# First mixer of a four-block trunk: u projected before the latents, S5 states beside the products of queries, keys and values

## Chip, cores, metric

One core of one Trainium2 chip. The metric is the device time of one execution in microseconds (us), the median of the runs shown.

## What is computed

Two layers, each a half-weighted feed-forward, a mixer, and another half-weighted feed-forward, on 256 tokens of width 1024. Only the mixer of layer 0 is changed. It projects the normalised input to u (512 columns), the query latent (384), the key and value latent (256) and a rotary key (32), and joins an S5 recurrence over u with a causal attention of 8 heads:

```python
def _even_mixer(h, cos_m, sin_m, w_in, ...):
    proj = h @ w_in
    u, c_q, c_kv, k_rope = jnp.split(proj, [S5_WIDTH, ...], axis=-1)
    s5_out = _s5(u, ...)      # states x_t = a x_{t-1} + B u_t; y = Re(C x) + D u; gelu, gate
    q = (_rmsnorm(c_q, q_norm) @ w_uq)...      # 8 heads of 64 + 32 rotary
    kv = (_rmsnorm(c_kv, kv_norm) @ w_ukv)...  # 8 heads of 64 + 64
    ...
    o = _causal_attention(q_full, k_full, v)
    return jnp.concatenate([s5_out, o], axis=-1) @ w_out
```

## The kernel before

Everything is float32, computed as three products of float32r halves: each operand is split into `hi` and `lo`, and hi·hi, hi·lo and lo·hi are summed in PSUM. Weights are split on the chip. `Weights.pre` (L54 to L73) makes one chunk: ScalarE (ACT) copies a staged piece to `whi` (L69), VectorE (DVE) subtracts it to get `wlo` (L71), and SyncE issues the load of a later piece (L50). In the first mixer there are four wide buffers, two chunks' worth, so a chunk can only be split once TensorE (PE) has finished with the chunk two places ahead of it in the list `mix0`.

The order on each engine is fixed when the program is built, by a scheduler that works from the order in which the code issues; at run time each engine takes its instructions in that order. The mixer `mixer0` issues, in this order:

- `cq` and `ckv`, the latents (48 products each), then `pu`, the projection of u (48 products). `low_rank` normalises the latents: a square with a sum on ACT, one step on DVE, a power on GpSimd (POOL), a product on DVE. `latents` transposes them between the two halves of `pu`.
- `queries(0)` and `keys_values(0)`: the products of heads 0 to 3 (18 on `pq`, 12 on `pk`), with u's blocks turned to the S5 layout between them (`uT`, `u`: 8 transposes on PE, copies on ACT and DVE).
- `block_inputs`: 32 products that bring u into the S5 states' space (`v_re`, `v_im`), for two halves b = 0 and 1 of the 16 pairs of S5 groups.
- `heads_turned(0)`: 16 transposes and the copies `qT` (DVE) and `kT` (ACT), without which no score can begin; then the first scores, and `states(b)` in pieces between `queries(1)`, `keys_values(1)` and the first two heads.
- `states(b)`: on DVE 6 products and sums, 2 scans and 3 more products and sums (`z_re`, `z_im`, `t`, `xs_re`); on POOL 3 operations (`xs_im`). `outputs(b)`: 24 products `yp` that need `xs_re` and `xs_im` of that half. `gelu(b)` follows, then the gate and the output projection.

`attend(h)` issues the scores of head h+2 and the values of head h: three transposes of the exponentials, a copy `pT` on ACT, three products.

Of the kernel before, what the change touches and what calls it, by code (L numbers as in the profile page):

```python
# [29 lines left out]
class Weights:  # L30
    """A stream of weight chunks: loaded ahead, each split exactly into two float32r parts."""
# [22 lines left out]
    def pre(self, other=None):  # L54
        """Splits the next chunk; other: an engine that helps with its second half."""
# [32 lines left out]
def trunk(ctx: ExitStack, tc: tile.TileContext, x, pos, invf, wff, gains, w_u, w_cq, w_ckv,  # L88
# [42 lines left out]
    def behind_both(last):  # L131
        """Work that is issued after two instructions on their engines."""
# [25 lines left out]
    mix0 = [(w, True) for w in (w_cq[0], w_cq[1], w_ckv[0], w_ckv[1], w_u[0], w_u[1], w_uq[0], w_ukv[0], w_uq[1],  # L158
# [9 lines left out]
    def rsqrt(out, a):  # L168
        """out = a ** -0.5, one column or more."""
        nc.gpsimd.tensor_tensor(out=out, in0=a, in1=mhalf[:, :a.shape[1]], op=ALU.pow)  # L170
# [13 lines left out]
    def transpose_split(src, nk, hi, lo, t):  # L184
        """token-major src [128, nk*128] -> feature-major halves, columns of token tile t."""
# [9 lines left out]
    # Phases hand the residual stream over one token tile at a time: a phase's last products for tile 0  # L195
    # come first, and those for tile 1 run while tile 0 is normalised for the next phase.
# [67 lines left out]
    def ffn(prev, row, background=None):  # L264
# [25 lines left out]
        # the first two feature tiles, one token tile at a time  # L290
# [73 lines left out]
    def sincos(ang, cos, sin, n, tmp):  # L364
        """cos and sin of ang [128, n] by an exact reduction to [-pi, pi]."""
# [19 lines left out]
    # exp by powf: its base is e rounded to float32, which a factor makes good  # L385
# [80 lines left out]
    def rope(v, nh, cc, ss, half, eng=None):  # L466
        """v [128, nh, 2*half] in place."""
# [27 lines left out]
    def s5_prep():  # L495
# [16 lines left out]
        # matrices that are filled last hold intermediates until then  # L512
# [21 lines left out]
        # powers of a and of its direction  # L534
# [21 lines left out]
        # e^{i theta n}, n = 0..63, by doubling  # L556
# [16 lines left out]
        # f = (a - 1) / lambda, bb = f B  # L573
# [31 lines left out]
        # inputs to states: E_i = a^{3-i} bb, and their transposes  # L605
# [22 lines left out]
        # states to outputs: W_d = c a^d  # L628
# [38 lines left out]
        # within a block: rows (i', c'), columns (i, c) hold Re(c a^{i-i'} bb), and the skip on the diagonal  # L667
# [12 lines left out]
    def product(acc, t, ws, k0, per, width, hi, lo, nk, cols=None):  # L680
        """token tile t of a product with k-tiles k0.. of the weights, `width` columns"""
# [18 lines left out]
    def row_maxima(sp, s, scale, mx):  # L700
        """masked and scaled scores of two query tiles, and the maxima of their rows"""
# [5 lines left out]
    def row_exps(s, mx, l):  # L707
        """exponentials and their sums; mx: the maxima, negated"""
# [13 lines left out]
    def mixer0(prev):  # L722
# [12 lines left out]
        cq = [bank("cq")[:, :384] for _ in range(2)]  # L735
        c0, c1 = queue.pop(0), queue.pop(0)
        product(cq[0], 0, c0, 0, 4, 384, yh, yl, KT)
        finish()
        product(cq[0], 0, c1, 4, 4, 384, yh, yl, KT)
        product(cq[1], 1, c0, 0, 4, 384, yh, yl, KT)  # L740
        more()
        product(cq[1], 1, c1, 4, 4, 384, yh, yl, KT)
        more()
        cqh, cql = s4("cqh", [128, 3, SEQ], F32R), s4("cql", [128, 3, SEQ], F32R)
        ckh, ckl = s2("ckh", [128, 2, SEQ], F32R), s2("ckl", [128, 2, SEQ], F32R)
        cqy = [low_rank(cq[t], 384, qg[:, :384]) for t in range(2)]
# [9 lines left out]

        ckv = [bank("ckv")[:, :288] for _ in range(2)]
        project(ckv, 288, lambda: None)
# [4 lines left out]

        # u, then blocks of four steps down the partitions
        pu = [bank("pu") for _ in range(2)]

        def latents():
            for t in range(2):
                transpose_split(cqy[t], 3, cqh, cql, t)
            for t in range(2):  # L770
                transpose_split(cky[t], 2, ckh, ckl, t)

        project(pu, 512, latents)
        us = [s2("us", [128, 512]) for _ in range(2)]
        for t in range(2):
            nc.scalar.copy(out=us[t], in_=pu[t])
# [5 lines left out]
        def queries(g):  # L782
# [7 lines left out]
            if g == 0:  # L790
                more()

        def keys_values(g):
# [7 lines left out]
            if g == 0:  # L801
                more()

        queries(0)
# [4 lines left out]
        uT = s4("uT", [128, 4, 4, NBLK])  # L809
        for t in range(2):  # L810
            pt = bank("pt").rearrange("p (k c) -> p k c", c=128)
            for k in range(4):
                nc.tensor.transpose(pt[:, k, :], us[t][:, k * 128:(k + 1) * 128], ident)
            pv = pt.rearrange("p m (n i) -> p m i n", i=4)
            for i in range(4):
                nc.scalar.copy(out=uT[:, :, i, 32 * t:32 * t + 32], in_=pv[:, :, i, :])
        u = s4("u", [128, NPAIR, NBLK])
        uv = u.rearrange("p (m a) n -> p m a n", a=4)
        for a in range(4):
            for i in range(4):  # L820
                dst = uv[32 * i:32 * i + 32, :, a, :]
                src = uT[32 * a:32 * a + 32, :, i, :]
                if i == 3 or i == 1 and a % 2:
                    nc.scalar.copy(out=dst, in_=src)
                else:
                    nc.vector.tensor_copy(out=dst, in_=src)
        keys_values(0)
# [45 lines left out]
        st = [states(b, *v[b]) for b in range(2)]  # L873
        s5e.close()
        att = ExitStack()
# [123 lines left out]
        next(st[0])  # L999
        queries(1)  # L1000
        attend(0)
        next(st[1])
        keys_values(1)
        attend(1)
        for _ in st[0]:
            pass
        heads_turned(1)
        for _ in st[1]:
            pass
        more()  # L1010
        yp = outputs(0)
        attend(2)
        gelu(0, yp)
        attend(3)
        osb = normalised(0)
        attend(4)
        yp = outputs(1)
# [349 lines left out]
```

## Time and profile before

| | us |
|---|---|
| median of 3 runs (1045.62 to 1045.81) | 1045.69 |
| span of the profiled execution, first to last instruction | 1044.7 |
| busy: PE, DVE, ACT, POOL | 1012.1, 635.2, 494.1, 101.4 |
| mean granted TensorE clock | 0.980 |

The profiled execution is of the same program; what of a run lies outside its span is some 1.0 us against the median. PE is busy for 97% of the span, so a shorter time has to come from its idle time or from stretches in which its clock is at the lower of its two levels.

### The profile page before, as it was taken

Reading aid. Unit: us, or ns where it says so; the run is one execution under the profiler, and the core shown is the slowest. Engines: PE = TensorE matmul, PEld = TensorE weight load, DVE = VectorE, ACT = ScalarE, POOL = GpSimd, SP = SyncE. Lnnn points to the kernel's source line nnn. Section 1 sums busy time; section 2 is a strip of 40 time slices with the busy share of each in tenths; the row PEclk is TensorE's granted clock in tenths of the full one; section 3 lists DMA queues with packets and bytes.
Section 4 is the critical chain, followed back from the end, with each engine's and each line's share of the span. In section 5 each row is a group of like instructions: output and inputs, shape, how many; then the busy total and the mean of one; then the engine's idle time right before and its main releaser. Section 6 shows DMA issues by size and latency. Waiting matters only on the chain.

```text
span 1044.7 us, 16739 instructions
## 1 busy us (share of the span) xinstructions
PE 1012.1 (97%) x6730; PEld 928.3 (89%) x6730; DVE 635.2 (61%) x1117; ACT 494.1 (47%) x848; POOL 101.4 (10%) x115
## 2 busy tenths in 40 slices
PE   7999998999979999999999999999999999999997
PEld 6999997989878899999989999999888879999996
DVE  5788778365877865555447455543757776555432
ACT  5454542455636664444336444442567756444431
POOL 3210006601510100000010000000101110000000
PEclk9999997899969999999999999999999999999999
DMA  8866663135113585555627565563453448556521
GB/s 270 262 186 196 189 190 101 51 117 187 61 41 111 192 302 182 182 184 186 209 68 263 168 217 185 189 190 140 143 180 122 143 133 290 184 184 192 187 80 40
DMA packets 49807, 174.93 MB, mean 167 GB/s; under 512 B 6081, under 2 KB 7105, under 8 KB 49730
## 3 DMA queue, kind: packets, MB, share of 16 engines
q1 hardware_dynamic: 48720, 170.46, 50.8%
q10 hardware_dynamic: 1010, 3.41, 0.9%
q8 instruction: 52, 0.85, 0.3%
q14 instruction: 25, 0.20, 0.1%
HBM read 172.80 MB, written 1.05 MB: 166 GB/s over the span
## 4 chain that ended last, share of the span: by engine, by line
PE 85%; DVE 6%; issue 3%; ACT 3%; POOL 1%; DMA 1%; SPq 0%; POOLq 0%; DVEq 0%; ACTq 0%
PE gu L336 43%; PE acc L280 22%; PE proj L685 6%; PE gt L300 3%; DVE wlo L71 2%; PE acc L696 2%; PE pu L685 1%; DVE tmat L118 1%; PE pt L190 1%; DMA xr<-in_x_dram 1%; PE ckv L685 1%; PE pz L976 1%; PE cq L685 1%; PE yp L944 1%; ACT y L199 1%
## 5 line engine op out<-in xcount | busy, mean ns | idle before, releaser
L71 DVE TENSOR_TENSOR wlo<-stage,whi 128x1024 fp32r<-128x1024 f32 x230 | 287.8, 1259 | 244.1 <-ACT whi L69 243.9
L69 ACT CAST whi<-stage 128x1024 fp32r<-128x1024 f32 (+1 forms) x236 | 240.4, 1030 | 292.5 <-issue 237.6
L336 PE MATMUL gu<-yh,whi 128*128 128x256 f32 x1280 | 363.1, 284 | 0.0
L336 PE MATMUL gu<-yh,wlo 128*128 128x256 f32 x1280 | 363.0, 284 | 0.0
L336 PE MATMUL gu<-yl,whi 128*128 128x256 f32 x1280 | 362.8, 283 | 0.0
L336 PEld LDWEIGHTS gu<-yh,whi 128*128 128x128 f32 x1280 | 246.2, 192 | 2.7
L336 PEld LDWEIGHTS gu<-yl,whi 128*128 128x128 f32 x1280 | 246.2, 192 | 2.7
L336 PEld LDWEIGHTS gu<-yh,wlo 128*128 128x128 f32 x1280 | 246.1, 192 | 0.0
L280 PE MATMUL acc<-dhi,hs 128*128 128x512 f32 x704 | 193.7, 394 | 0.0
L280 PEld LDWEIGHTS acc<-dhi,hs 128*128 128x128 f32 x704 | 128.1, 190 | 23.3 <-ACT hs L127 0.3
L71 DVE TENSOR_TENSOR dlo<-stage,dhi 128x1024 fp32r<-128x1024 f32 x88 | 108.3, 1232 | 36.3 <-ACT dhi L69 35.8
L69 ACT CAST dhi<-stage 128x1024 fp32r<-128x1024 f32 x88 | 92.3, 1050 | 68.8 <-DMA stage<-in_wff_dram 68.6
L280 PE MATMUL acc<-dlo,hs 128*128 128x512 f32 x352 | 110.9, 391 | 0.0
L280 PEld LDWEIGHTS acc<-dlo,hs 128*128 128x128 f32 x352 | 66.4, 189 | 14.4
L170 POOL TENSOR_TENSOR rs<-rs,mhalf 128x1 f32<-128x1 f32 x14 | 7.8, 557 | 658.4 <-DVE rs L124 658.4
L118 DVE TENSOR_TENSOR sh<-sh,gu 128x256 f32<-128x256 f32 x80 | 33.1, 414 | 31.8 <-ACT sh L340 31.8
L118 DVE TENSOR_TENSOR hs<-sh,hs 128x256 fp32r<-128x256 f32 x80 | 35.6, 445 | 18.7 <-ACT hs L127 18.6
L340 ACT ACTIVATE sh<-gu 128x256 f32<-128x256 f32 x80 | 30.3, 379 | 31.3 <-PE gu L336 31.3
L127 ACT CAST hs<-sh 128x256 fp32r<-128x256 f32 x80 | 32.3, 403 | 16.9 <-DVE sh L118 16.9
L685 PE MATMUL proj<-whi,yh 128*128 128x512 f32 x96 | 38.7, 403 | 0.2 <-ACT yh L127 0.2
L685 PE MATMUL proj<-wlo,yh 128*128 128x512 f32 x96 | 37.5, 391 | 0.0
L300 PE MATMUL gt<-whi,yh 128*128 128x256 f32 x128 | 34.7, 300 | 2.7 <-ACT yh L127 2.6
(326 smaller groups left out, 1138.7 us busy)
## 6 DMA issues: line engine op xcount, KB each, us to landing
stage<-in_wff_dram SPq DMA_DIRECT2D x264, 512.0 KB, 4.6
stage<-in_w_in_dram SPq DMA_DIRECT2D x24, 512.0 KB, 4.4
stage<-in_w_out_dram SPq DMA_DIRECT2D x16, 512.0 KB, 3.7
gain<-in_gains_dram ACTq DMA_DIRECT2D x6, 512.0 KB, 4.9
stage<-in_w_u_dram SPq DMA_DIRECT2D x4, 512.0 KB, 4.7
xr<-in_x_dram SPq DMA_DIRECT2D x2, 512.0 KB, 5.2
stage<-in_w_cq_dram SPq DMA_DIRECT2D x2, 512.0 KB, 4.1
stage<-in_w_ckv_dram SPq DMA_DIRECT2D x2, 512.0 KB, 4.7
```

Of the source, the lines that this page charges most:

```text
L69: nc.scalar.copy(out=hi[:, c:c + w], in_=t[:, :w])
L71: eng.tensor_tensor(out=lo[:, c:c + w], in0=t[:, :w], in1=hi[:, c:c + w].bitcast(F32), op=ALU.subtract)
L118: return nc.vector.tensor_tensor(out=out, in0=a, in1=b, op=op)
L127: copy = nc.scalar.copy(out=hi, in_=src)
L190: nc.tensor.transpose(pt[:, k, :], src[:, (k0 + k) * 128:(k0 + k + 1) * 128], ident)
L199: return nc.scalar.activation(out=y[:, sl], in_=xr[t][:, sl], func=AF.Square, scale=1.0 / 32.0, accum_out=ms[:, c:c + 1]).ins
L280: nc.tensor.matmul(acc[t][c], a[:, sl], w[:, c * 512:(c + 1) * 512], start=(f == 0 and n == 0), stop=(f == NF - 1 and n == 2))
L300: last = nc.tensor.matmul(o, a[:, k, sl], w[:, k * 256:(k + 1) * 256], start=(k0 == 0 and n == 0), stop=(k0 > 0 and n == 11))
L336: nc.tensor.matmul(gu[:, s * 256:(s + 1) * 256], w[:, k, s, :], a[:, k, :], start=(k == 0 and n == 0), stop=(k == KT - 1 and n == 2))
L340: nc.scalar.activation(out=sh[:, 0, :], in_=gu[:, :256], func=AF.Silu)
L685: last = nc.tensor.matmul(acc, a[:, k0 + k, sl], w[:, k * width:(k + 1) * width], start=(k0 == 0 and n == 0), stop=(k0 + per == nk and n = ...
L696: mm = nc.tensor.matmul(acc[t][c], a[:, k0 + k, sl], w[:, o:o + 512], start=(first and k == 0 and n == 0), stop=(last and k == 1 and n == 2))
```

## The change

No arithmetic is changed. In `mix0` the chunks of u come first. `mixer0` projects u where it projected the query latent, turns u's blocks between the two halves of the `cq` product (`u_blocks`), and turns the query latents between the two halves of the `ckv` product. `block_inputs` then follow the latents, before any query or key product. `states(0)` is issued between `queries(0)` and `keys_values(0)`, `states(1)` between `queries(1)` and `keys_values(1)`, each whole, and only after all of these `heads_turned(0)`. The two calls of `more()` that split the first output chunk and the gate's chunk move up into `queries(1)` and `keys_values(1)`. `outputs(b)` and `gelu(b)` are issued between the first heads. The comments and docstrings that the full difference also removes are left out here.

```diff
-    mix0 = [(w, True) for w in (w_cq[0], w_cq[1], w_ckv[0], w_ckv[1], w_u[0], w_u[1], w_uq[0], w_ukv[0], w_uq[1],
+    mix0 = [(w, True) for w in (w_u[0], w_u[1], w_cq[0], w_cq[1], w_ckv[0], w_ckv[1], w_uq[0], w_ukv[0], w_uq[1],
...
-        cq = [bank("cq")[:, :384] for _ in range(2)]
+        pu = [bank("pu") for _ in range(2)]
         c0, c1 = queue.pop(0), queue.pop(0)
-        product(cq[0], 0, c0, 0, 4, 384, yh, yl, KT)
+        product(pu[0], 0, c0, 0, 4, 512, yh, yl, KT)
         finish()
...
+        cq = [bank("cq")[:, :384] for _ in range(2)]
+        project(cq, 384, u_blocks)
+        cqy = [low_rank(cq[t], 384, qg[:, :384]) for t in range(2)]
...
         ckv = [bank("ckv")[:, :288] for _ in range(2)]
-        project(ckv, 288, lambda: None)
+        project(ckv, 288, query_latents)
...
-            if g == 0:
-                more()
+            more()
...
         v = [block_inputs(b) for b in range(2)]
-        st = [states(b, *v[b]) for b in range(2)]
         s5e.close()
+        for t in range(2):
+            transpose_split(cky[t], 2, ckh, ckl, t)
+        queries(0)
+        for _ in states(0, *v[0]):
+            pass
+        keys_values(0)
+        queries(1)
+        for _ in states(1, *v[1]):
+            pass
+        keys_values(1)
...
         heads_turned(0)
         sc = {0: scores(0), 1: scores(1)}
-        next(st[0])
-        queries(1)
-        attend(0)
-        next(st[1])
-        keys_values(1)
-        attend(1)
-        for _ in st[0]:
-            pass
         heads_turned(1)
-        for _ in st[1]:
-            pass
-        more()
-        yp = outputs(0)
-        attend(2)
-        gelu(0, yp)
-        attend(3)
-        osb = normalised(0)
-        attend(4)
-        yp = outputs(1)
-        heads_out(0, osb)
-        more()
-        attend(5)
-        gelu(1, yp)
+        attend(0)
+        yp = outputs(0)
+        attend(1)
+        gelu(0, yp)
+        attend(2)
+        yp = outputs(1)
+        attend(3)
+        osb = normalised(0)
+        gelu(1, yp)
+        attend(4)
+        heads_out(0, osb)
+        attend(5)
         halves(gh, gl, gt)
```

DVE's order before, from the copies of u's blocks to the first piece of `states(0)` (`z_re`, `z_im` and `t` are tiles of the states, `wlo` is a half of a weight chunk, here that of heads 4 to 7's keys and values):

```order
L826 COPY u<-uT 32x4x64 x10
L118 TENSOR_TENSOR z_re<-v_re,cosn 128x512
L118 TENSOR_TENSOR t_3002<-v_im,sinn 128x512
L71 TENSOR_TENSOR wlo<-stage,whi 128x1024
L890 COPY qT<-pt 96x4x128 x2
L118 TENSOR_TENSOR z_re<-z_re,t_3002 128x512
L118 TENSOR_TENSOR z_im<-v_im,cosn 128x512
```

And DVE's order now, from the halves of the key latents to the middle of `states(0)`; the first two `wlo` rows belong to the chunk of `queries(1)`, whose buffers `queries(0)` gives back:

```order
L118 TENSOR_TENSOR ckl<-pt,ckh 128x2x128 x2
L71 TENSOR_TENSOR wlo<-stage,whi 128x1024
L71 TENSOR_TENSOR wlo<-stage,whi 128x128
L118 TENSOR_TENSOR z_re<-v_re,cosn 128x512
L118 TENSOR_TENSOR t_2918<-v_im,sinn 128x512
L118 TENSOR_TENSOR z_im<-v_im,cosn 128x512
L118 TENSOR_TENSOR z_re<-z_re,t_2918 128x512
L71 TENSOR_TENSOR wlo<-stage,whi 128x1024
L118 TENSOR_TENSOR t_2918<-v_re,sinn 128x512
```

Before, two `qT` copies stood behind the first two operations of `states(0)`; now none stands here, and `states(0)` stands behind a chunk that waits for `queries(0)`.

Where DVE's `qT` copies of the first four heads stand now: at the end of `states(1)`, from its first scan on (the `wlo` row is the second piece of the gate's chunk, the L703 row the maxima of the first scores):

```order
L847 SCALAR_TENSOR_TENSOR z_re<-mag_115,z_re 128x512
L118 TENSOR_TENSOR z_im<-z_im,t_3004 128x512
L118 TENSOR_TENSOR xs_re<-z_re,cosn 128x8x63
L847 SCALAR_TENSOR_TENSOR z_im<-mag_115,z_im 128x512
L71 TENSOR_TENSOR wlo<-stage,whi 128x1024
L118 TENSOR_TENSOR t_3004<-z_im,sinn 128x8x63
L896 COPY qT<-pt 96x4x128
L118 TENSOR_TENSOR xs_re<-xs_re,t_3004 128x8x63
L896 COPY qT<-pt 96x4x128
L703 ISA s,mx_3094<-sp,mask 128x128
```

All but the last step of both halves' states, and seven weight pieces, now stand between the block inputs and the first `qT` copy.

PE's order now at the same place, from the last key product (`pk`) to the first scores (`sp`), which need `qT`:

```order
L685 MATMUL pk<-whi,ckl 128x512 x2
L893 MATMUL pt<-ident,q_sb 96x128 x4
L893 MATMUL pt<-ident,kfull 96x128 x4
L893 MATMUL pt<-ident,q_sb 96x128 x4
L893 MATMUL pt<-ident,kfull 96x128 x4
L906 MATMUL sp<-kT,qT 128x128 x2
L893 MATMUL pt<-ident,q_sb 96x128
L907 MATMUL sp<-kT,qT 128x256 x2
```

Before, the same 16 transposes stood directly behind the block inputs, and `queries(1)` and `keys_values(1)` behind the first scores; now all products of queries, keys and values stand ahead of the transposes.

## Rows read from the trace of the kernel before

**Rows 1.** The page: span, and busy time of each engine.

```profile
span 1044.7 us, 16739 instructions
PE 1012.1 (97%) x6730; PEld 928.3 (89%) x6730; DVE 635.2 (61%) x1117; ACT 494.1 (47%) x848; POOL 101.4 (10%) x115
```

**Rows 2.** Waits of PE from 226 to 330 us: total, times, longest.

```profile
PE yp L944 <- DVE xs_re L118: 5.4, 1, 5.4
PE po L916 <- ACT pT L718: 1.5, 2, 0.9
PE pt L190 <- DVE y L121: 0.6, 2, 0.3
PE yp L943 <- DVE t L118: 0.5, 1, 0.5
PE pz L976 <- DVE gl L118: 0.4, 1, 0.4
```

**Rows 3.** Stretches of 1 us: busy PE, PEld, DVE, ACT, POOL; then granted clock.

```profile
289.00:290.00 1.00, 0.00 (x0) 0.00 (x0) 1.00 (x1) 0.00 (x0) 0.85 (x1) 0.69 0.00 0
290.00:291.00 1.00, 0.00 (x0) 0.00 (x0) 1.00 (x2) 0.00 (x0) 0.00 (x0) 0.50 0.00 0
306.00:307.00 1.00, 1.00 (x9) 0.91 (x9) 0.66 (x3) 0.54 (x1) 0.00 (x0) 0.78 0.06 16
307.00:308.00 1.00, 1.00 (x8) 0.63 (x6) 0.79 (x5) 0.53 (x2) 0.00 (x0) 1.00 0.00 0
```

**Rows 4.** PE in order of time: start, duration, instructions, [idle before <- releaser].

```profile
237.94 0.29 PE L685 MATMUL ckv<-whi,yh 128*128 128x288 f32 x1
...
256.45 0.33 PE L685 MATMUL pq<-whi,cqh 128*128 128x384 f32 x1
...
259.60 1.03 PE L813 MATMUL pt<-ident,us 128*128 128x128 f32 x8
260.39 0.47 PE L685 MATMUL pk<-whi,ckh 128*128 128x512 f32 x1
...
263.23 0.36 PE L838 MATMUL v_re<-u,e_re 128*128 128x64 f32 x2
...
270.69 0.60 PE L887 MATMUL pt<-ident,q_sb 128*96 128x128 f32 x4
...
272.43 0.67 PE L900 MATMUL sp<-kT,qT 96*128 96x128 f32 x4
...
292.92 0.69 PE L944 MATMUL yp<-xs_re,w_re 128*128 128x64 f32 x2 [5.41 <-DVE xs_re L118]
```

**Rows 5.** DVE in order of time, the same columns.

```profile
240.69 0.62 DVE L121 SCALAR_TENSOR_TENSOR cy<-cq,rs,qg 128x384 f32<-128x384 f32 x1 [0.66 <-POOL rs L170]
...
261.97 3.36 DVE L826 COPY u<-uT 32x256 f32<-32x256 f32 x10
268.28 0.69 DVE L118 TENSOR_TENSOR z_re<-v_re,cosn 128x512 f32<-128x512 f32 x1 [2.94 <-PE v_re L838]
...
269.48 1.22 DVE L71 TENSOR_TENSOR wlo<-stage,whi 128x1024 fp32r<-128x1024 f32 x1
271.32 0.69 DVE L890 COPY qT<-pt 96x512 f32<-96x512 f32 x1 [0.62 <-PE pt L887]
...
275.86 1.22 DVE L850 TENSOR_TENSOR_SCAN z_re<-mag,z_re 128x512 f32<-128x512 f32 x1
...
284.69 1.73 DVE L118 TENSOR_TENSOR t<-z_im,sinn 128x504 f32<-128x504 f32 x1
...
295.70 0.67 DVE L118 TENSOR_TENSOR t<-z_im,sinn 128x504 f32<-128x504 f32 x1
```

**Rows 6.** DVE, products and sums of both states alone (L118), 268 to 298.2 us.

```profile
268.00:298.20 30.20, 14.63 (x18) 0.85 0.05 18
```

**Rows 7.** DVE, scans of both states alone (L850), same stretch.

```profile
268.00:298.20 30.20, 5.82 (x4) 0.85 0.05 18
```

**Rows 8.** All engines, same stretch; the columns of Rows 3.

```profile
268.00:298.20 30.20, 23.39 (x149) 21.48 (x148) 28.27 (x49) 11.89 (x31) 13.60 (x14) 0.85 0.05 18
```

More of the change, by code (lines that the diff above doesn't have):

```diff
@@ L734, in mixer0, with u_blocks @@
         nc.scalar.activation(out=small("warm", 1), in_=mhalf[:, :1], func=AF.Exp)
-        cq = [bank("cq")[:, :384] for _ in range(2)]
+        pu = [bank("pu") for _ in range(2)]
         c0, c1 = queue.pop(0), queue.pop(0)
-        product(cq[0], 0, c0, 0, 4, 384, yh, yl, KT)
+        product(pu[0], 0, c0, 0, 4, 512, yh, yl, KT)
         finish()
-        product(cq[0], 0, c1, 4, 4, 384, yh, yl, KT)
-        product(cq[1], 1, c0, 0, 4, 384, yh, yl, KT)
+        product(pu[0], 0, c1, 4, 4, 512, yh, yl, KT)
+        product(pu[1], 1, c0, 0, 4, 512, yh, yl, KT)
         more()
-        product(cq[1], 1, c1, 4, 4, 384, yh, yl, KT)
+        product(pu[1], 1, c1, 4, 4, 512, yh, yl, KT)
         more()
+        us = [s2("us", [128, 512]) for _ in range(2)]
+        for t in range(2):
+            nc.scalar.copy(out=us[t], in_=pu[t])
+        uT = s4("uT", [128, 4, 4, NBLK])
+        u = s4("u", [128, NPAIR, NBLK])
+        def u_blocks():
+            for t in range(2):
+                pt = bank("pt").rearrange("p (k c) -> p k c", c=128)
+                for k in range(4):
+                    nc.tensor.transpose(pt[:, k, :], us[t][:, k * 128:(k + 1) * 128], ident)
+                pv = pt.rearrange("p m (n i) -> p m i n", i=4)
+                for i in range(4):
+                    nc.scalar.copy(out=uT[:, :, i, 32 * t:32 * t + 32], in_=pv[:, :, i, :])
+            uv = u.rearrange("p (m a) n -> p m a n", a=4)
+            for a in range(4):
+                for i in range(4):
+                    dst = uv[32 * i:32 * i + 32, :, a, :]
+                    src = uT[32 * a:32 * a + 32, :, i, :]
+                    if i == 3 or i == 1 and a % 2:
+                        nc.scalar.copy(out=dst, in_=src)
+                    else:
+                        nc.vector.tensor_copy(out=dst, in_=src)
         cqh, cql = s4("cqh", [128, 3, SEQ], F32R), s4("cql", [128, 3, SEQ], F32R)
         ckh, ckl = s2("ckh", [128, 2, SEQ], F32R), s2("ckl", [128, 2, SEQ], F32R)
-        cqy = [low_rank(cq[t], 384, qg[:, :384]) for t in range(2)]
         def project(acc, width, between):
@@ L755, in project, with query_latents @@
                     between()
+        cq = [bank("cq")[:, :384] for _ in range(2)]
+        project(cq, 384, u_blocks)
+        cqy = [low_rank(cq[t], 384, qg[:, :384]) for t in range(2)]
+        def query_latents():
+            for t in range(2):
+                transpose_split(cqy[t], 3, cqh, cql, t)
         ckv = [bank("ckv")[:, :288] for _ in range(2)]
-        project(ckv, 288, lambda: None)
+        project(ckv, 288, query_latents)
         cky = [low_rank(ckv[t][:, :256], 256, qg[:, 384:]) for t in range(2)]
@@ L762, in mixer0 @@
             nc.scalar.copy(out=kpe[:, t, :], in_=ckv[t][:, 256:288])
[L765 to L776, printed above, removed]
         q_sb = [s4("q_sb", [128, 8, 96]) for _ in range(2)]
@@ L800, in keys_values @@
                 nc.scalar.copy(out=v_sb[:, t, 256 * g:256 * g + 256], in_=pk[t][:, 1])
-            if g == 0:
-                more()
-        queries(0)
+            more()
         for t in range(2):
@@ L808, in mixer0 @@
             nc.gpsimd.tensor_copy(out=kfull[t][:, :, 64:96], in_=kv.to_broadcast([128, 8, 32]))
[L809 to L827, printed above, removed]
         xs_re, xs_im = s4("xs_re", [128, NPAIR, NBLK]), s4("xs_im", [128, NPAIR, NBLK])
@@ L872, in mixer0 @@
         v = [block_inputs(b) for b in range(2)]
-        st = [states(b, *v[b]) for b in range(2)]
         s5e.close()
+        for t in range(2):
+            transpose_split(cky[t], 2, ckh, ckl, t)
[7 more added lines that the diff above has]
+        keys_values(1)
         att = ExitStack()
@@ L998, in mixer0 @@
         sc = {0: scores(0), 1: scores(1)}
-        next(st[0])
-        queries(1)
+        heads_turned(1)
         attend(0)
-        next(st[1])
-        keys_values(1)
+        yp = outputs(0)
         attend(1)
-        for _ in st[0]:
-            pass
-        heads_turned(1)
-        for _ in st[1]:
-            pass
-        more()
-        yp = outputs(0)
+        gelu(0, yp)
         attend(2)
-        gelu(0, yp)
+        yp = outputs(1)
         attend(3)
         osb = normalised(0)
+        gelu(1, yp)
         attend(4)
-        yp = outputs(1)
         heads_out(0, osb)
-        more()
         attend(5)
-        gelu(1, yp)
         halves(gh, gl, gt)
```

## The prediction

> **What bounds the kernel now.** I read the page first: PE is busy for 1012 of 1044.7 us [rows 1], so nothing outside PE's path pays unless it makes PE wait or lowers its clock. Then I read the waits of PE in the first mixer. One stands out, 5.4 us of the S5 outputs for `xs_re` on DVE; the others are 1.5 us for `pT`, 0.6 us for the normalised input, 0.5 us for the states' buffers and 0.4 us for the gate's input [rows 2]. Third, the granted clock: it falls to 0.69 and then 0.50 while PE waits, the lower of its two levels (1.2 of 2.4 GHz), and is back at 1.00 only after 306 us [rows 3]. PE resumes at 292.92 [rows 4] and the 0.78 of the stretch 306 to 307 puts the return near 306.4, so PE works 13.4 us at half its clock, which costs 6.7 us. What the S5 states cost the path now is thus 5.4 + 0.5 + 6.7 = 12.6 us, and that is what the change could give back.
>
> Last, who keeps `xs_re` late. DVE is busy for 28.3 of the 30.2 us from 268 to 298.2 [rows 8]: it is the bound of that stretch, and its order decides what PE gets first. Before, `qT` goes in between the pieces of `states(0)`: the first copy starts at 271.32, PE's first scores at 272.43, and PE has products of queries and keys to do while DVE works on the states [rows 4, 5].
>
> **The change, part by part.** The number of products on PE is the same, and so is the arithmetic on DVE, ACT and POOL. So the sum is one of waits: those removed, those added, and the time at half clock.
>
> *Up to the first keys.* Before, the last of cq, ckv, u, `queries(0)`, `keys_values(0)` and the block inputs is done when the heads' transposes begin, at 270.69 [rows 4]. After, the same work ends with `keys_values(0)`. Three things make it later. (a) The u chunks that are split at the end of the feed-forward have 1024 columns in their second piece and not 512, half a piece more on DVE, some 0.5 us, ahead of the last hidden halves; nothing to 0.5, I take 0.2. (b) The 8 transposes of y's second tile stand together, with no product between them; that place costs PE 0.3 us now, half of the 0.6 [rows 2], and I take 0.3 more (0 to 0.7, a second half of y's product). (c) The query latents are turned after half of the ckv product, not after half of u's. Now the second `cy` starts 2.75 us after the cq product has ended (240.69 against 237.94) and takes 0.62 [rows 4, 5], 3.4 us in all; half of ckv lasts some 3.2 us (18 products of 384 columns, the pq group below, take 3.15 us; 24 of 288 columns are as many). But the ten copies of u's blocks (3.36 us on DVE [rows 5]) now stand ahead of the latents' steps and end at about the end of cq, so the first `cy` and a split of 1.3 us come behind them. I take a wait of 1.0 us (0.2, if the copies are done earlier, to 2). Together 1.5 us: `keys_values(0)` ends at 272.2. One pk group lasts 263.23 - 260.39 = 2.84 us and one pq group 259.60 - 256.45 = 3.15 us [rows 4]; `queries(0)` therefore ends at 269.4.
>
> *When DVE begins the states.* This is the term that decides. v of the first half is there from about 262, as the block inputs precede `queries(0)`. But ahead of the first `z_re` DVE's order has both pieces of the chunk of `queries(1)`, and these go into the buffers of the chunk that `queries(0)` reads. Now the same split is over 261.97 - 259.60 = 2.4 us after `queries(0)` has ended [rows 4, 5]. After, `states(0)` can begin at 271.8, 9 us after its data are there. DVE has idle time then, but stands at a wait, and everything behind it waits too.
>
> *How long until `qT`.* Both states now take 14.6 us of products and sums and 5.8 us of scans [rows 6, 7], less about 1.0 us in which neighbours overlap: 19.4 us. Five splits of 1.14 us (1.22 in [rows 5], less 0.08 of overlap) make 5.7 us, two `qT` copies of 0.61 us 1.2 us. In all 26.3 us: the second copy is done at 298.1, the first at 296.9 (the last step of the states, 0.6, and the second copy, 0.6, come behind it). Bounds: without POOL beside it each of the 18 products takes 0.60 (0.67 less overlap) and each scan 1.14 (1.22 less overlap) [rows 5], 15.4 us instead of 19.4, and `qT` comes 4.0 us earlier; the upper bound is a rival below.
>
> *PE's new wait.* After `keys_values(0)` PE has 3.15 + 2.84 us of products and the 16 transposes, 272.43 - 270.69 = 1.74 us [rows 4], and is done at 279.9. The first scores need the first `qT` copy: PE waits from 279.9 to 296.9, **17.0 us**. Nothing covers it: behind the scores stand the rest of the heads and `outputs(0)`, all in PE's order behind them. ACT waits for maxima that DVE has not begun, so it has nothing to give either.
>
> *The clock.* A wait of 5.4 us is followed by 13.4 us at half clock now [rows 3, 4]. I take the same 13.4 us after the longer wait, from 296.9 to 310.3: another 6.7 us lost, as much as before, so this term is nil.
>
> *The rest of the heads.* The same products follow. Added: 0.6 us for the first head's `pT`, which now has no products beside it, and about 1.0 us for the fifth, whose copy on ACT stands behind the square of `gelu(1)` (0 to 2 in all). `outputs(0)` and `outputs(1)` no longer wait, as the states are done by 298. The gate's input is ready in time, because `gelu(1)` comes two heads earlier. The two splits that moved up cost PE nothing here; their price is in the 26.3 us.
>
> *Sum.* Added 1.5 + 17.0 + 0.6 + 1.0 = 20.1 us; removed 5.4 + 0.5 + 1.5 + 0.4 = 7.8 us; clock 0. Net 12.3 us. PE now changes less often between scores and products of queries and keys, and at a change the first product runs longer (0.47 us for the first pk [rows 4]); I put that at 1 us back, an estimate. So +11.3 us on the median of 1045.7: **1057.0 us**. The span of the profiled execution, 1044.7, would become 1056.0.
>
> *A rule weighed.* `t<-z_im,sinn` takes 1.73 us at 284.69 and 0.67 at 295.70 [rows 5], the first of them beside POOL's half of the states; POOL is busy for 13.6 us of that stretch [rows 8] and costs DVE 19.4 - 15.4 = 4.0 us. The Trainium skill (SBUF — State Buffer, Who interferes with whom) says that a VectorE instruction with two inputs in SBUF and a GpSimd instruction that reads SBUF exclude each other: whoever starts first keeps the other fully blocked. By that rule at its strictest all of POOL's time would fall on DVE, and the wait would be longer by about 10 us; the rows show a share of it, since POOL is as often the one that waits.
>
> **Rivals.** *The clock counts from the last pause.* If the 13.4 us start anew at PE's short pause for the first `pT`, some 8.6 us after it resumed, half clock lasts 8.6 us longer and costs 4.3 more: 1061.3. For it: before, no wait fell into the 13.4 us. Against: the pause is short, 0.6 us.
>
> *POOL's whole time on DVE.* 15.4 + 13.6 us of states instead of 19.4, and PE waits 9.6 us longer: 1066.6. Against it speak the 4.0 us that POOL costs now.
>
> *POOL and DVE miss each other*, the lower bound, 4.0 us less: 1053.0. For it: in `states(0)` POOL also has the rotary steps, which now come earlier; against: POOL's three operations follow the scans as before.
>
> *The states are hidden, and the time falls.* If DVE gave `qT` when PE has turned the heads, at about 280, there would be no wait of 17.0 us and no half clock: 1057.0 - 17.0 - 6.7 = 1033.3. For it: DVE now stands idle for 2.94 us ahead of its first `z_re` [rows 5]. It decides where DVE needs less than 26.3 - 11.3 = 15 us from the end of that split to `qT`: more than that and the wait still eats what the outputs' wait gives back. Against it: 15.4 us of states at the very least, with 5.7 us of splits among them.
>
> *The change does little*, because the products now beside the states make up for the late scores: it would need `qT` within 1 us or two of those 15 us. The same rows speak against it.
>
> **Chances and range.** The forecast, with a wait of 15 to 19 us, 0.62; clock 0.16; POOL's whole time 0.04; POOL and DVE apart 0.10; hidden 0.05; little 0.03. 0.2% of the time, 2.1 us, is about what a measurement of this kernel can tell from no change. So faster 0.05, same 0.03, slower 0.92. The cases of 1053 to 1061, with an error of 3 us at both ends for (a) to (c), the heads and the changes of product, give the range 1050 to 1064, and leave out 0.12.
>
> **What would show it.** On DVE, `z_re` starts behind the split for `queries(1)`, near 272, with the idle time ahead of the split; the first `qT` starts near 296. On PE one wait for `qT` (line 906) of about 17 us from 280 on, and no wait of the S5 outputs for `xs_re`; the clock at 0.50 from about 282 until 310. Should `z_re` start near 262, or `qT` stand in the trace before 290, the central step is wrong. If the wait is there and the time is not longer, the heads behind it gave back more than I counted.

## The result, and the profile after

The changed kernel takes 1058.28 us (median of 13 runs, 1055.04 to 1059.99). The kernel before, run beside it, takes 1047.53 us (median of 13). The ratio is 1.0079, with a 95% interval of 1.0053 to 1.0105: the change is slower by 5.5 to 11 us. Executions of one kernel differ in how long TensorE's clock stays at its lower level (five of the 13 of the kernel before took 1054.6 to 1057.0 us); the mean granted clock of an execution stands beside its time where it matters, and ratios leave out executions that are over 1.5% above the fastest of their kernel (of the interleaved kernel below, five of ten).

The page of the changed kernel answers [rows 1]: DVE and POOL are busy for 0.8 and 1.7 us longer, PE for 4.9 us less, and the span is 10.3 us longer.

```profile
span 1055.0 us, 16735 instructions
PE 1007.2 (95%) x6730; PEld 923.1 (88%) x6730; DVE 636.0 (60%) x1117; ACT 493.0 (47%) x848; POOL 103.1 (10%) x115
```

The waits of PE in the first mixer, 226 to 345 us, stand against [rows 2] (line, what it waited for, engine; total, times, longest):

```profile
PE sp L906 <- DVE qT L896: 18.9, 1, 18.9
PE pt L716 <- ACT s L710: 1.6, 1, 1.6
PE po L922 <- ACT pT L718: 1.2, 2, 0.6
PE pt L190 <- DVE cy L121: 0.8, 1, 0.8
PE pt L190 <- DVE y L121: 0.7, 1, 0.7
```

The outputs no longer wait for `xs_re`; the first scores wait 18.9 us for `qT`. The kernel before has two short waits beside those of [rows 2]:

```profile
PE pt L716 <- ACT s L710: 0.3, 1, 0.3
PE v_re L838 <- ACT u L824: 0.2, 1, 0.2
```

So the waits were 8.9 us; now these five and one more of 0.2 make 23.4.

DVE in order of time, against [rows 5]:

```profile
266.70 0.76 DVE L118 TENSOR_TENSOR ckl<-pt,ckh 128x256 fp32r<-128x256 f32 x2 [3.66 <-ACT ckh L127]
270.23 1.69 DVE L71 TENSOR_TENSOR wlo<-stage,whi 128x1024 fp32r<-128x1024 f32 x2 [2.77 <-ACT whi L69]
271.85 0.68 DVE L118 TENSOR_TENSOR z_re<-v_re,cosn 128x512 f32<-128x512 f32 x1
...
277.69 1.75 DVE L118 TENSOR_TENSOR xs_re<-z_re,cosn 128x504 f32<-128x504 f32 x1
...
283.27 1.47 DVE L71 TENSOR_TENSOR wlo<-stage,whi 128x1024 fp32r<-128x1024 f32 x1
...
298.18 0.68 DVE L896 COPY qT<-pt 96x512 f32<-96x512 f32 x1
298.78 1.13 DVE L118 TENSOR_TENSOR xs_re<-xs_re,t 128x504 f32<-128x504 f32 x1
299.83 0.67 DVE L896 COPY qT<-pt 96x512 f32<-96x512 f32 x1
```

The low halves of the key latents (`ckl`) and the split for `queries(1)` stand ahead of `z_re`, each with idle time in front of it, and `qT` stands behind all of `states(0)` and nearly all of `states(1)`. PE's order of time shows the other end of that wait, and stretches of 4 us (busy PE, PEld, DVE, ACT, POOL, then the granted clock) answer [rows 3]:

```profile
299.00 1.19 PE L906 MATMUL sp<-kT,qT 96*128 96x128 f32 x4 [18.95 <-DVE qT L896]
```

```profile
280.00:284.00 4.00, 0.05 (x1) 0.00 (x0) 4.00 (x4) 1.84 (x3) 3.34 (x3) 0.93 0.31 92
284.00:288.00 4.00, 0.00 (x0) 0.00 (x0) 3.88 (x5) 0.00 (x0) 4.00 (x7) 0.50 0.48 170
...
300.00:304.00 4.00, 3.75 (x14) 2.83 (x13) 2.58 (x12) 0.99 (x4) 0.00 (x0) 0.51 0.02 4
304.00:308.00 4.00, 3.43 (x29) 3.10 (x28) 1.63 (x8) 3.32 (x11) 0.00 (x0) 1.00 0.00 0
```

A mean of 0.51 over 300 to 304 puts the return of the clock at 303.9, 4.9 us after PE resumed. In the kernel before it took 13.4 us of work [rows 3, 4]. The ledger of the span: the waits of the mixer are 23.4 - 8.9 = 14.5 us longer, and one wait at 12 us, where nothing was changed, happens to be 0.7 us longer in this execution (2.6 against 1.9); together 15.2. PE is busy for 1012.1 - 1007.2 = 4.9 us less, of which (13.4 - 4.9) / 2 = 4.3 us are the clock's. 15.2 - 4.9 makes the 10.3 us by which the spans differ.

### The profile page after: what moved, and what is told of

Read it like the earlier page. It is cut to its first block, busy times and chain, and to the rows that moved or that the text cites. A ratio compares the mean times of both kernels' runs of the same rounds, so it can differ in the third digit from the quotient of the medians.

```text
span 1055.0 us, 16735 instructions
## 1 busy us (share of the span) xinstructions
PE 1007.2 (95%) x6730; PEld 923.1 (88%) x6730; DVE 636.0 (60%) x1117; ACT 493.0 (47%) x848; POOL 103.1 (10%) x115
## 4 chain that ended last, share of the span: by engine, by line
PE 84%; DVE 7%; issue 4%; ACT 3%; POOL 1%; DMA 1%; SPq 0%; DVEq 0%; POOLq 0%; ACTq 0%
PE gu L336 43%; PE acc L280 21%; PE proj L685 6%; PE gt L300 3%; DVE wlo L71 2%; PE acc L696 2%; PE pu L685 1%; DVE tmat L118 1%; DMA xr<-in_x_dram 1%; PE pt L190 1%; ACT y L199 1%; PE pz L982 1%; ACT s L710 0%; DVE w_im L118 0%; PE sp L1121 0%
## 5 line engine op out<-in xcount | busy, mean ns | idle before, releaser
L118 DVE TENSOR_TENSOR sh<-sh,gu 128x256 f32<-128x256 f32 x80 | 33.1, 413 | 31.8 <-ACT sh L340 31.8
L118 DVE TENSOR_TENSOR hs<-sh,hs 128x256 fp32r<-128x256 f32 x80 | 35.5, 444 | 16.2 <-ACT hs L127 16.2
```

Of the source, the lines that this page charges most:

```text
L118: return nc.vector.tensor_tensor(out=out, in0=a, in1=b, op=op)
```

## The experiments

Theory: DVE takes its instructions in order; `qT` is late because it stands behind a split that must wait for `queries(0)`, then behind both states and the other pieces. Rivals: what is late is not the order but the sum of DVE's work with POOL beside it; or the clock.

**The wait is in DVE's order: take the copies off, start the states earlier, move pieces back.** The edits to the changed kernel:

```diff
 # qT_on_act: heads_turned
-                    if src is q_sb:
-                        nc.vector.tensor_copy(out=d, in_=pt[:96])
-                    else:
-                        nc.scalar.copy(out=d, in_=pt[:96])
+                    nc.scalar.copy(out=d, in_=pt[:96])
 # states0_early
+        st = states(0, *v[0])
+        next(st)
         for t in range(2):
             transpose_split(cky[t], 2, ckh, ckl, t)
         queries(0)
-        for _ in states(0, *v[0]):
+        for _ in st:
             pass
 # pieces_later: the pieces of queries(1) and keys_values(1)
-            more()
+            if g == 0:
+                more()
...
         attend(1)
+        more()
         gelu(0, yp)
...
         yp = outputs(1)
+        more()
```

> The changed kernel with one edit: the copies of the turned queries (qT) are made by ACT, as those of the keys are, instead of by DVE. Theory (DVE's queue): TensorE waits 18.9 us for qT because the copies stand in DVE's order behind both states and the weight pieces; take the copies off DVE and the wait is not gone but moves on by one link, to the maxima of the first scores, which stand in DVE's order at the same place. The first row maximum began at 301.88 us in the changed kernel and can begin when the states' product before it ends, about 298.2: a gain of 3 to 4 us, span about 1051.5, and TensorE's long wait is then at the transposes of the exponentials, for ACT's s. Rival (the copies themselves, or what they read, are late): with the copies on an idle engine the wait of 18.9 us goes nearly whole, span about 1037 to 1040.

> The changed kernel with the first half of the first states (eight operations on DVE, up to the scans) written ahead of the turning of the key latents, so that in DVE's order it stands ahead of the weight piece that has to wait for the first queries. Theory (DVE's queue, in order): DVE is idle for 8 of the 11 us before 270.2 us while the states' inputs are ready at 264.6; the first half (about 6.5 us) fills that hole, all that follows comes 6 to 7 us earlier, the first qT copy at about 292 instead of 298.2, TensorE's wait for it 12 to 13 us instead of 18.9, and at most 1 us is lost where the keys wait for the latents' low halves. Span 1048 to 1050, 5 to 7 us less than the changed kernel. Rival (what is late is not DVE's order but the sum of the states' work beside POOL, or the pieces' buffers): the first half comes earlier and DVE then waits at its next piece; the qT copies stay within 1.5 us of where they were, span 1053 to 1055.

> The changed kernel with two splits of weight chunks (those behind the second queries and the second keys and values) put where they were written in the kernel before, between the heads. Theory (DVE's queue): three pieces of 1.2 to 1.5 us leave the queue ahead of the qT copies, and the copies come up between the operations of the second states; the second part of the first scores then starts about 7 us earlier, but the first maxima still stand behind the last two operations of the states and begin at about 297 instead of 301.88. 4 to 5 us less than the changed kernel, span about 1050.5, part of the wait now shown at the exponentials. Rival (the pieces fill time in which DVE would stand anyway): no change, span 1054 to 1056.

| kernel | median, lowest to highest, us (runs) | mean clock | ratio to before, 95% |
|---|---|---|---|
| qT_on_act | 1066.56, 1062.35 to 1071.50 (6) | 0.963 to 0.975 | 1.0173, 1.0129 to 1.0217 |
| states0_early | 1054.34, 1053.34 to 1054.94 (12) | 0.980 to 0.983 | 1.0055, 1.0034 to 1.0076 |
| pieces_later | 1058.00, 1056.38 to 1065.82 (7) | 0.968 to 0.975 | 1.0102, 1.0060 to 1.0144 |

The longest waits of PE in these three, in that order:

```profile
PE pt L716 <- ACT s L710: 9.8, 2, 8.2
PE pt L893 <- POOL q_sb L473: 5.1, 1, 5.1
```

```profile
PE sp L908 <- DVE qT L898: 13.9, 1, 13.9
```

```profile
PE sp L908 <- DVE qT L898: 8.7, 1, 8.7
PE pt L716 <- ACT s L710: 3.8, 2, 2.4
```

And in the second of them, the first step of the states on DVE:

```profile
261.50 0.68 DVE L118 TENSOR_TENSOR z_re<-v_re,cosn 128x512 f32<-128x512 f32 x1
```

The chain went as the theory has it, each time: without the copies on DVE the wait stands one link on, at the exponentials, whose maxima are on DVE (and 5.1 us of wait for POOL's rotation of the queries came up beside it); with the first half of the states in the idle hole it is 5.0 us shorter; with three pieces fewer ahead of `qT`, and the copies moved up between the operations of `states(1)`, 10.2 us shorter. The time went along only in the second case, by 3.9 us, where 5 to 7 were expected. The clock says why. In the kernel with the pieces later, stretches of 2 us (this execution is one of the two of seven that took over 1065 us; the other five took 1056.4 to 1058.9 at a mean clock of 0.974 or 0.975):

```profile
294.00:296.00 2.00, 0.00 (x0) 0.00 (x0) 2.00 (x11) 0.27 (x1) 1.59 (x2) 0.76 0.00 0
296.00:298.00 2.00, 1.16 (x3) 0.47 (x3) 2.00 (x9) 1.98 (x9) 0.00 (x0) 0.50 0.00 0
...
334.00:336.00 2.00, 2.00 (x10) 1.71 (x9) 0.20 (x1) 0.58 (x1) 0.00 (x0) 0.50 0.00 0
336.00:338.00 2.00, 2.00 (x17) 1.73 (x15) 1.97 (x7) 1.60 (x4) 0.00 (x0) 1.00 0.00 0
```

The long wait is halved, but the clock falls a second time at the 2.4 us for `s` and stays at 0.50 from 295.0 to 336.0, with PE busy for nearly all of it. In the kernel with the copies on ACT it is at 0.50 from 284.5 to 291.4, with work from 287.8 on, and from 298.2 to 318.7, with work from 301.2 on. So the expected 3 to 5 us fell to the clock, and more: these two expectations missed the time.

**POOL beside DVE.** The changed kernel, with `xs_im` made by DVE:

```diff
-                nc.gpsimd.tensor_tensor(out=out, in0=x, in1=y, op=op)
+                tt(out, x, y, op)
```

> The changed kernel with the three operations on each of the two states that POOL makes (xs_im) made by DVE. Theory (collision): DVE's operations of 0.6 us beside them took 1.73 us, five of them, one 1.13, and two weight pieces 0.3 us too long, 6.4 us in all; six operations of 0.6 us more are 3.6 us. The second qT copy comes about 2.8 us earlier (297.0 instead of 299.8), no operation of the states takes more than 0.7 us apart from the scans, span about 1052. Rival (those operations are slow for a reason of their own, as their shape or the scans beside them): they keep their 1.73 us, and the added work makes the wait longer by 3.6 us or more, span 1058 to 1060.

Measured 1056.37 us (1055.54 to 1059.02, 10 runs; clock 0.977 to 0.980), ratio 1.0066 (1.0033 to 1.0099): some 2 us less than the changed kernel by the medians, with ranges that overlap. DVE's products and sums alone (L118), 268 to 301 us, first in this kernel, then in the changed one:

```profile
268.00:301.00 33.00, 15.69 (x24) 0.70 0.33 112
```

```profile
268.00:301.00 33.00, 17.26 (x18) 0.73 0.34 111
```

Twenty-four operations at 0.654 us take less than eighteen beside POOL. At 0.654 the eighteen would be 11.8 us, so by this estimate POOL costs DVE 5.5 us there, not the 4.0 that I took from the kernel before. The rival of operations that are slow of themselves fails. The expected size did not come, though: DVE's first step of the states and its `qT` copies,

```profile
270.44 0.68 DVE L118 TENSOR_TENSOR z_re<-v_re,cosn 128x512 f32<-128x512 f32 x1
295.95 1.28 DVE L896 COPY qT<-pt 96x512 f32<-96x512 f32 x2
```

are 26.8 us apart from start to end, and 28.65 in the changed kernel: 1.9 us less, where 2.8 were expected. Beside POOL's rotation of the queries five products still take 0.75 to 0.93.

**The clock alone.** Transposes of the identity that nothing reads, where PE waits: 160 ahead of the first scores of the changed kernel; 45 and 70 in the kernel with the copies on ACT; 46 ahead of the first outputs of the kernel before.

```diff
+        idle = bank("idle")
+        for _ in range(160):
+            nc.tensor.transpose(idle[:, :128], ident, ident)
```

> The changed kernel with 160 transposes of the identity into a bank of its own, which nothing reads, put in TensorE's order where it waits 18.9 us for qT; nothing else changes. By the changed kernel's rows they take about 0.11 us each, 17.4 us in all, and end before qT is there. Theory (the clock's share): the granted clock stays at 1.00 through the wait, the 4.6 us that TensorE worked at half clock after it are saved by half, and the rest of the loss stays, since DVE sets the end of the wait: 2 to 3 us less, span 1052 to 1053. Rival (the wait's price is mostly the clock): 6 us or more less. If the added products hold DVE up, the wait's end moves later.

> The kernel with the qT copies on ACT, with 45 and 70 transposes of the identity, which nothing reads, where TensorE waited 5.1 us for the second queries and 8.2 us for the exponentials. Theory (that kernel lost by the clock, not by the copies): its granted clock was 0.50 from about 299 to 318 us, against 284 to 304 with only 4.6 us of work in it in the changed kernel; kept busy, TensorE stays at 1.00, and what is left is the earlier first maximum (about 300 instead of 301.88): span 1050 to 1053, at least 8 us less than that kernel, and 2 to 4 less than the changed one. Rival (ACT's copies hold the chain up): it stays within 4 us of the kernel with the copies on ACT, span 1057 or more.

> The kernel before with 46 transposes of the identity, which nothing reads, where TensorE waited 5.4 us for the first states (xs_re) ahead of the first S5 outputs; they take some 5.0 us and end before the states do; nothing else changes. Theory (the clock's price of a short wait): the wait itself stays, since DVE sets its end, but the granted clock, which the profile of the kernel before shows at 0.50 for 13.4 us of work behind it, stays at 1.00: 6 to 7 us less, span 1038, and none of the executions at 1054 to 1057 us that the kernel before also has. Rival (the clock falls for the shorter waits around it too): the times stay where the kernel before has them, 1045 to 1048 us with some 8 us longer.

| kernel | median, lowest to highest, us (runs) | mean clock | ratio to before, 95% |
|---|---|---|---|
| pe_kept_busy | 1058.40, 1055.84 to 1059.87 (10) | 0.984 to 0.989 | 1.0058, 1.0024 to 1.0091 |
| act_kept_busy | 1069.33, 1061.54 to 1070.43 (4) | 0.971 to 0.980 | 1.0158, 1.0088 to 1.0227 |
| before_busy | 1053.14, 1051.36 to 1055.05 (12) | 0.977 to 0.982 | 1.0036, 1.0011 to 1.0062 |

None gained. The sizes expected for the first and the last came neither by the theory nor by the rival; the second stayed within 4 us of the kernel with the copies on ACT, as its rival has it. The first, in order of time and in stretches:

```profile
278.13 17.63 PE L1006 MATMUL idle<-ident 128*128 128x128 f32 x160
297.31 0.46 PE L906 MATMUL sp<-kT,qT 96*128 96x128 f32 x2 [1.55 <-DVE qT L896]
298.96 1.19 PE L907 MATMUL sp<-kT,qT 96*128 96x256 f32 x2 [1.19 <-DVE qT L896]
```

```profile
292.00:296.00 4.00, 3.76 (x35) 3.52 (x33) 4.00 (x4) 0.00 (x0) 2.25 (x2) 1.00 0.06 9
296.00:300.00 4.00, 1.50 (x5) 1.18 (x6) 2.82 (x4) 0.00 (x0) 1.60 (x2) 0.78 0.37 124
...
304.00:308.00 4.00, 3.43 (x24) 3.07 (x22) 1.50 (x6) 2.69 (x10) 0.00 (x0) 0.87 0.00 0
```

The clock holds through the filled wait, falls at 298.2, at the next two short ones, and is back at 305.0: 6.1 us of work at half clock, against 4.9 in the changed kernel, only later. With the copies on ACT it falls at 301.6, behind waits of 1.1 and 0.8 us, until 339.1. The longest waits of the kernel before with the added products:

```profile
PE po L916 <- ACT pT L718: 3.3, 2, 2.4
PE pt L716 <- ACT s L710: 2.4, 1, 2.4
```

There the clock holds past the outputs and is then at 0.50 from 302.7 to 323.2, at the two waits of 2.4 us for `s` and `pT`, where the longest were 0.3 and 0.9 us; the added products also changed the scheduler's order (two splits and a step of `gelu` stand ahead of maxima on DVE), so that this run does not price the clock alone. The 6.7 us at half clock were not to be had back in this way: where PE came sooner, DVE was late for it.

**The order of the products alone.** The kernel before with u projected first, the latents then, the rest in its old place:

```diff
-    mix0 = [(w, True) for w in (w_cq[0], w_cq[1], w_ckv[0], w_ckv[1], w_u[0], w_u[1], w_uq[0], ...
+    mix0 = [(w, True) for w in (w_u[0], w_u[1], w_cq[0], w_cq[1], w_ckv[0], w_ckv[1], w_uq[0], ...
...
         queries(0)
...
+        for t in range(2):
+            transpose_split(cky[t], 2, ckh, ckl, t)
         keys_values(0)
```

> The kernel before with one part of the change alone: u is projected first and the latents then (the chunks in that order, the key latents turned just ahead of the first keys); the states, the heads and the weight pieces stay where the kernel before has them. Theory (the loss comes from where the states stand, not from the order of the products): only the later first transposes (1.15 us in the changed kernel) and the wait for the second query latent (0.8) are paid, and the long waits of the kernel before stay; 1.5 to 2.5 us more than before, span about 1046.5. Rival (the order of the products is what costs, since the latents now come late): 6 us or more above the kernel before.

Measured 1056.18 us (1047.73 to 1058.25, 10 runs), ratio 1.0023 (0.9981 to 1.0066): inconclusive as a whole, since three runs were at a mean clock of 0.982 and seven at 0.970 to 0.975. The kernel before has the same two kinds; of its 25 runs there, 12 took 1045.6 to 1048.3 us at 0.980 to 0.983, and 13 took 1053.9 to 1057.0 at 0.971 to 0.974. At 0.982 the new order takes 1047.7 to 1048.8, about 1.5 to 2 us more: the size expected, and far from the rival's 6. The mechanism expected is not what the trace shows (of the slowest execution, 1058 us at 0.970): PE's longest waits are

```profile
PE pk L685 <- DVE ckl L118: 3.6, 2, 2.1
PE po L914 <- ACT pT L718: 3.5, 3, 1.6
```

so it waits for the key latents' low halves, now turned just ahead of the keys, and neither for `xs_re` nor for the second query latent. What the size consists of at 0.982 is open.

**Take DVE's queue apart.** From here on the order of the changed kernel's second half is rewritten. `interleaved`, then what the others add:

```diff
 # interleaved: states0_early, and
         queries(1)
-        for _ in states(1, *v[1]):
-            pass
-        keys_values(1)
...
         heads_turned(0)
         sc = {0: scores(0), 1: scores(1)}
+        st = states(1, *v[1])
+        next(st)
+        keys_values(1)
         heads_turned(1)
         attend(0)
+        for _ in st:
+            pass
         yp = outputs(0)
 # interleaved_busy: in heads_turned, between the token tiles
+                if t:
+                    idle = bank("idle")
+                    for _ in range(13):
+                        nc.tensor.transpose(idle[:, :128], ident, ident)
 # outputs_fill: the rest of states(0) behind heads_turned(0), and
         keys_values(1)
+        yp = outputs(0)
         heads_turned(1)
...
-        yp = outputs(0)
 # outputs_fill_later: the same, with the edit of pieces_later
```

> The changed kernel with the queue of DVE taken apart: the first half of the first states ahead of the key latents' turning, the first heads turned and two scores made before the second states begin, the second keys and values and the second turning beside the first half of the second states, its second half behind the first head. Theory (DVE's queue, in order): the qT copies of the first heads stand behind one state and four pieces only and are done at about 280, when TensorE comes to them; the wait of 18.9 us becomes 2 to 4 us, and no more than 4 us of new waits come up behind the second states; span 1036 to 1042, faster than both kernels. Rival (DVE's work with POOL beside it is a bound whatever the order): the wait comes back at the maxima or at the second turning, and the clock with it; span 1046 to 1053.

> The interleaved kernel with 13 transposes of the identity, which nothing reads, between the two token tiles of each turning of heads, where TensorE waited 1.4 and 1.7 us; nothing else changes. The interleaved kernel has no wait for qT left, and its times lie between 1040.2 and 1059.6 us, with the granted clock of the whole between 0.990 and 0.967: in its profile the clock fell at 287.5, just behind those two waits, and came back only at 331.5, 44 us of work at half clock. Theory (the clock alone is what is left, and these waits bring it down): with them filled the clock holds in most executions, median 1040 to 1044, none above 1053. Rival (the clock falls for another reason than these waits): times spread as before the filling, median above 1050.

> The interleaved kernel with the first S5 outputs (24 products, 5.3 us, which need only the first states) made between the second keys and values and the second turning, that is where TensorE waited for the second queries' rotation and keys; the rest of the first states is written behind the first turning, so that POOL rotates the queries first. Theory (order): real work stands in the waits, which fall from 5.7 us to under 3, span 1036 to 1040 where the clock holds, and it holds oftener. Rival (the outputs themselves have to wait for POOL's xs_im, which now comes later): the wait only changes its name, 2 us or more at the outputs, and the clock falls as in the interleaved kernel, 1050 to 1058.

> The same with the two weight chunks behind the second queries and the second keys split later, between the heads, as in the kernel before. Theory (order): two chunks less on ACT and DVE between 272 and 290 us bring the rotated keys' copies and the maxima forward by 1 to 3 us; 1 to 2 us faster than the kernel with the outputs alone, at the same clock. Rival (nothing waits for those pieces there any more): the same within 0.5 us.

| kernel | median, lowest to highest, us (runs) | mean clock | ratio to before, 95% |
|---|---|---|---|
| interleaved | 1054.34, 1040.20 to 1059.61 (10) | 0.967 to 0.990 | 0.9974, 0.9916 to 1.0032 |
| interleaved_busy | 1047.89, 1040.76 to 1060.35 (12) | 0.970 to 0.990 | 0.9973, 0.9934 to 1.0012 |
| outputs_fill | 1046.28, 1041.78 to 1048.82 (12) | 0.980 to 0.988 | 0.9961, 0.9932 to 0.9990 |
| outputs_fill_later | 1037.22, 1036.16 to 1038.19 (6) | 0.988 | 0.9884, 0.9845 to 0.9923 |

The interleaved kernel's longest waits, and its clock:

```profile
PE pt L892 <- POOL q_sb L473: 1.7, 2, 1.4
PE pt L892 <- ACT kfull L817: 1.7, 1, 1.7
PE po L921 <- ACT pT L718: 1.2, 2, 0.6
```

```profile
284.00:288.00 4.00, 1.96 (x14) 1.44 (x13) 4.00 (x15) 3.37 (x12) 0.95 (x3) 0.92 0.20 79
288.00:292.00 4.00, 3.43 (x15) 2.73 (x13) 4.00 (x4) 2.02 (x4) 1.62 (x1) 0.50 0.00 0
...
328.00:332.00 4.00, 4.00 (x17) 3.60 (x17) 3.63 (x13) 2.53 (x7) 0.00 (x0) 0.54 0.00 0
```

By order alone the wait for `qT` is gone from a list that shows nothing over 1.7 us, so the rival of DVE's sheer work fails as to the wait. The time is then the clock's: this execution, one of 1058 us, is at 0.50 from 287.4 to 331.7; the two at 0.988 and 0.990 took 1041.7 and 1040.2, so the 1036 to 1042 that were expected came in two of ten. Filling two of the short waits with transposes (the scheduler moved some DVE steps with it) brings 4 of 12 runs to 1040.8 to 1042.1, 4 to 1047.4 to 1048.1, and leaves 4 at 1053 to 1060: no cure, and a median between what theory and rival have. With the first outputs as filler, the rival's wait came:

```profile
PE yp L948 <- POOL xs_im L867: 2.0, 1, 2.0
```

Its median, 1046.3 us, again lies between the two. With two chunks less to split beside it, no wait of the mixer is over 0.8 us, and the mean clock is 0.988 in all six runs. Its page, its three longest waits from 226 to 350 us (the first belongs to the next feed-forward, where the kernel before has it too), and 276 to 308 us:

```profile
span 1034.9 us, 16736 instructions
```

```profile
PE gt L300 <- DVE wlo L71: 1.8, 1, 1.8
PE po L921 <- ACT pT L718: 1.3, 2, 0.8
PE pt L190 <- DVE y L121: 0.9, 2, 0.7
```

```profile
276.00:308.00 32.00, 29.85 (x230) 27.10 (x228) 29.94 (x81) 20.20 (x56) 10.98 (x13) 1.00 0.26 87
```

DVE is busy for 29.9 of those 32 us, much as in [rows 8], and PE for 29.9 too. It is 0.8 to 1.6% faster than the kernel before. The last expectation, 1 to 2 us, missed by 7, for it took the clock to be the same: with these pieces later the mean clock is 0.988 in every run, with them early in one of twelve.

## Why the prediction was right, and where its sizes were off

- **Up to the first keys**, forecast +1.5 us: the keys end at 272.2 as forecast, but by other parts, and in part by luck. The transposes of y start 1.15 us later (227.83 against 226.68), yet 0.7 of that is the longer wait at 12 us, which is no work of the change; in the other traces of kernels with u first they start anywhere from 226.0 to 227.9. What comes back in each of these traces is the wait in front of them, 0.66 to 0.68 us against 0.31: so (a) is some 0.4. (b) gives 0.3 back, for the second tile's transposes no longer wait, and (c) adds 0.8 instead of 1.0.
- **When DVE begins the states**, forecast 271.8: 271.85. In the kernel with the first half earlier it is 261.5, 8.9 us sooner when counted from the transposes of y (226.34 there). The forecast had only the split in front of the states. The changed kernel's rows show two links: DVE stands 3.7 us for `ckl`, which ends at 267.5, and only then 2.8 us for the split, so about half of the 8.9 us is the split's.
- **How long until `qT`**, forecast 26.3 us to the end of the second copy: 28.65. The term mis-sized is POOL's collision: 4.0 forecast, 5.5 on the products by the estimate above, and some 0.5 more on two splits that take 1.47 and 1.48 instead of 1.2. The Trainium skill (SBUF — State Buffer, Who interferes with whom) has the two exclude each other; the trace agrees in that only products with both inputs in SBUF are slow (`xs_re` 1.75, `z_re` from PSUM 0.68), but DVE bears 5.5 us of the 11.4 that POOL's six operations take, so the strictest reading, the rival of 1066.6, does not hold. POOL pays too: its second product of each half takes 2.15 us here and 1.25 in the kernel before.
- **PE's new wait**, forecast 17.0: 18.9, by that same term. Shown by its going when the order alone is changed.
- **The clock**, forecast nil (13.4 us at half clock again): mis-sized by 4.3 us. Only 4.9 us of work were at half clock. That the sum came within 1 us of the 10.3 of the spans is luck: the waits for `qT` were 2.1 us too short in it, those of the heads 1.2, and the clock's 4.3 us, which it had at nothing, hid them.
- **The rest of the heads**, forecast 1.6 us: 2.8, namely 1.2 for `pT` and 1.6 for `s`. **What is removed** (7.8 us): as forecast. Of the 1.0 us for fewer changes of product nothing was tested alone; PE's busy time fell by 0.6 us beside the clock's 4.3.
- **Rivals.** That the states could be hidden (1033.3) is not what this change does, but is near what its pieces allow: the last kernel takes 1037.2. The rival in which a later pause keeps the clock down did not come here. Longer stretches at half clock did come, in the kernel with the pieces later, in both with the copies on ACT and in the interleaved one; that a later pause is what kept it down there is not shown.

What is not settled: why one execution of the interleaved kernel keeps the clock and another loses it for 44 us. The runs show that it happens, and that of the last four kernels the one with the shortest waits is free of it in all six runs, not what decides it.

## What to carry over

An instruction that waits in an in-order queue holds all that stands behind it, so a move is judged by what comes to stand behind which wait: here the first states, which could begin some 9 us sooner, stood behind the key latents' halves and one split. Look at the time at which the consumer needs the last link, and put that link, not the bulk, first in the queue; give the waiting engine real work, and take optional work (weights for later) out of that stretch. And a wait is not priced by its length: halving it paid nothing where the clock fell for longer.

## What the runs showed of the hardware

TensorE's clock, once down at 0.50, came back 4.9 us after PE resumed in the changed kernel, 5.3 us with the states earlier, 13.4 us in the kernel before, and 40 and 44 us in the traces of the kernel with the pieces later and of the interleaved one, with PE busy by the profile for 38.4 and 43.1 us of these. It fell in a wait of 18.9 us and in one of 2.4 us alike, and behind two of 1.1 and 0.8 us that followed a filled one. The same program took 1040.2 and 1059.6 us, at mean clocks of 0.990 and 0.967.
